# Attention value products with the exponentials as the held operand, in a hybrid Fourier, attention and delta-rule layer

## The chip, the cores and the metric

The kernel runs on one core of a Trainium2 chip. The metric is the device time of one execution in microseconds; several runs are made, and their median is the kernel's time. Engines are called by their roles: TensorE (PE, with its weight loads as PEld), VectorE (DVE), ScalarE (ACT), GpSimd (POOL) and SyncE (SP), which here issues nearly all DMAs.

## The reference, cut to what matters

One layer of a generator on 1024 latent positions and 256 context positions, width 1024, all in float32. A combined input projection feeds a Fourier group, a group of 8 query heads on 2 key/value heads, and a Gated DeltaNet group; the three are concatenated into one output projection, and a squared-ReLU MLP follows. The change touches the attention group alone:

```python
def _attend(q, k, v):
    B, L, _, D = q.shape
    nb = L // QBLK
    qb = q.reshape(B, nb, QBLK, ATT_HKV, ATT_GROUP, D).transpose(1, 0, 2, 3, 4, 5)
    scale = D ** -0.5

    def blk(qi):
        s = jnp.einsum('bqhgd,bkhd->bhgqk', qi, k, preferred_element_type=jnp.float32) * scale
        p = jax.nn.softmax(s, axis=-1).astype(v.dtype)
        return jnp.einsum('bhgqk,bkhd->bqhgd', p, v)
...
    k_all = jnp.concatenate([P['ak'], Pc['ak']], axis=1)
    v_all = jnp.concatenate([P['av'], Pc['av']], axis=1)
    o_att = _attend(P['aq'], k_all, v_all)
```

There are 1024 queries and 1280 keys per head, with 64 channels.

## The kernel before

Most products run in a reduced-precision float32 type with operands split in a high and a low part, so that a product of full precision is a sum of two or three products. `rbase` and the `z1a`, `z1c`, `z2b` zones hold such operands in SBUF, `fbase` and the other zones plain float32; the PSUM banks are `A3` (three, `ba` in the profile) and `bk` (five).

The kernel goes through stages in order of program: modulation and input projection, the delta-rule systems, the attention steps, the output projection, and the MLP's two products (by a seven-product scheme). Attention is a loop of `NPR * 5` = 160 steps. There are 32 query groups `j` of 256 queries (4 groups for each of 8 heads, `h = j // 4`), and each has 5 steps `k2` of two key blocks of 128 keys. A step `n` runs, in this order:

- `side()`, from step `FIRST` = 2 to `LATE` = 145: one piece of other work, first the delta rule's scan (`scan`, many products of 32 or 64 rows on `bk[3]` and `bk[4]`), then the Fourier group (`spectra`);
- `values(n)`: the value products of this step, added up over the 5 steps in the bank `pvs[j % 2]` (`A3[2]` or `bk[2]`);
- `scores(n + LA)`, three steps ahead: four score products, the exponential on ScalarE, and its split into a high part (ScalarE) and a low part (VectorE or GpSimd) in `hl`, with keys on partitions;
- a piece of `maxima` (row maxima for the group two further on), now and then the transposes of `q_T` and `k_T`, and one entry of the list `later`;
- at `k == 4`, `finish(j)`.

In `values`, `VH` and `VL` (the values' high and low parts, 64 channels and a column of ones or zeros) are held, and the exponentials move: high and low side by side in one product of 512 columns on `VH`, the high part alone in one of 256 columns on `VL`. The output has channels on partitions, 0 to 63, and the sum of exponentials on partition 64. `finish` adds the two halves and sends the row of sums to memory; `divide` (after each pair of heads, and after each query group of the last pair) fetches the sums back spread over partitions, takes reciprocals, stores them, fetches them back broadcast, and puts the multiplies and splits into `later`. The result goes to `catAr`, channels on partitions, for the output projection.

A scheduler orders each engine's instructions with its own estimate of times; while `pinned` is set, which holds for all attention steps, TensorE's products and transposes stay in the order of the program (`pe`). `mm` issues one product, `tp` one transpose (a product with the identity).

Of the kernel before, what the change touches and what calls it, by code (L numbers as in the profile page):

```python
# [10 lines left out]
F32 = mybir.dt.float32  # L11
# [3 lines left out]
ALU = mybir.AluOpType  # L15
AX = mybir.AxisListType

P = 128
D = 1024
S = 1024  # L20
# [3 lines left out]
NT = S // P  # L24
NCT = CTX // P
NTA = NT + NCT
HD = 64
CK = 32
VC_ = 68
NCL = S // CK  # L30
NCC = CTX // CK
NCA = NCL + NCC
# [11 lines left out]
PIN = lambda i: i  # L44
# [3 lines left out]
DEFER = 4  # L48
# [143 lines left out]
def body(tc, t, out):  # L192
# [3 lines left out]
    with ctx:  # L196
# [11 lines left out]
        dram = ctx.enter_context(tc.tile_pool(name="scratch", bufs=1, space=bass.MemoryType.DRAM))  # L208
# [4 lines left out]
        def buf(*shape, top=False, a=None, at=None):  # L213
            return Buf(a or Fa, (P,) + shape, top, at)

        def rbuf(*shape, a=None):
            return Buf(a or Ra, (P,) + shape)

        def act(o, i, f=AF.Copy, **k):
            return SC.activation(o, i, f, **k)  # L220

        def f32(ap):
            return ap.bitcast(F32)
# [8 lines left out]
        def mm(o, l, r, start, stop):  # L232
            pe(T.matmul(o, l, r, start=start, stop=stop))  # L233
# [6 lines left out]
        def tp(o, i):  # L240
            pe(T.transpose(o, i, C["ident"]))
# [173 lines left out]
        for k, _ in enumerate(mod_steps(0, slabs, bk[2])):  # L415
            b = trb.next()
# [247 lines left out]
        b = gb.next()  # L664
# [236 lines left out]


        catA = [rbuf(4, S) for _ in range(2)]
        ab = dict(identr=rbuf(P), vlh=rbuf(NTA, 2, VC_), mr=[rbuf(2, VC_) for _ in range(2)], kv=buf(NTA, 2, HD), q=[buf(NT, HD) for _ in range(2)], p=[buf(512) for _ in range(2)], st=[buf(8) for _ in range(6)])
        qr, pr, str_, mrr = (Ring(ab[k]) for k in ("q", "p", "st", "mr"))
        ptr_ = Ring([bk[0], bk[1]])
        ld = [[dram.tile([2, S], F32, name=f"l{w}{q}") for q in range(4)] for w in "ab"]
        catAr = [b() for b in catA]
        VH, VL = (ab["vlh"]()[:, :, w, 0 : HD + 1] for w in range(2))
        identr = ab["identr"]()  # L910
        V.tensor_copy(identr, C["ident"])
        for m_ in ab["mr"]:
# [9 lines left out]
        V.tensor_copy(VH[:, :, HD], C["ones"][:, 0:NTA])  # L922
        V.tensor_scalar(VL[:, :, HD], C["ones"][:, 0:NTA], 0.0, None, op0=ALU.mult)
        s1r = Ring(A3[0:2])
        pvs = [A3[2], bk[2]]
        KVr = ab["kv"]()
# [73 lines left out]

        def values(n):
            k2, hl, pv = n % 5, pt.pop(n), pvs[n // 5 % 2]
            for kk in range(2):
                kb = k2 * 2 + kk
                if kb == 9:
                    mm(pv[0 : HD + 1, 0:256], VL[:, kb], hl[:, kk, 0], False, False)
                mm(pv[0 : HD + 1], VH[:, kb], hl[:, kk].rearrange("p a b -> p (a b)"), kb == 0, kb == 9)
                if kb < 9:
                    mm(pv[0 : HD + 1, 0:256], VL[:, kb], hl[:, kk, 0], False, False)

        def finish(j):
            h, gq = j // 4, j % 4
            if j % 8 == 0:
                o2[h // 2] = o2r.next()()
            O2 = o2[h // 2]
            r = slice(64 * (h % 2), 64 * (h % 2) + 64)
            cs_ = slice(gq * 256, gq * 256 + 256)
            o1, lr = o1r.next()(), lrr.next()()
            pv = pvs[j % 2]
            act(o1[0:65], pv[0:65, 256:512])  # L1020
            V.tensor_tensor(O2[r, cs_], pv[0:64, 0:256], o1[0:64], op=ALU.add)
            V.tensor_tensor(lr[64:65], pv[64:65, 0:256], o1[64:65], op=ALU.add)
            la, lb_ = (x[h // 2] for x in ld)
            Y.dma_start(la[h % 2 : h % 2 + 1, cs_], lr[64:65])

            def divide(n, c0, eng, pin=pe):
                li, rl = lir.next()()[0 : n // 8], rlr.next()()[:, c0 : c0 + n]
                zs = slice(c0, c0 + n)
                Y.dma_start(li, la[:, zs].rearrange("h (p q) -> h p q", q=16))
                V.reciprocal(li, li)  # L1030
                Y.dma_start(lb_[:, zs].rearrange("h (p q) -> h p q", q=16), li)
                for z in range(2):
                    Y.dma_start(rl[64 * z : 64 * z + 64], lb_[z : z + 1, zs].to_broadcast([64, n]))
                for c in range(c0, c0 + n, 256):
                    cs_, ch, cl = slice(c, c + 256), *(x[:, h // 2, c : c + 256] for x in catAr)

                    def mul(cs_=cs_, ch=ch, c=c):
                        pin(eng.tensor_tensor(O2[:, cs_], rl[:, c - c0 : c - c0 + 256], O2[:, cs_], op=ALU.mult))
                        (pe if n < S else PIN)(act(ch, O2[:, cs_]))

                    def sub(cs_=cs_, ch=ch, cl=cl):
                        pin(eng.tensor_tensor(cl, O2[:, cs_], f32(ch), op=ALU.subtract))

                    later.extend((mul, sub))

            if j // 4 == NPR // 4 - 1:
                later.extend([None] * DEFER)
                divide(256, gq * 256, V)
            elif j % 8 == 7:
                later.extend([None] * 5)  # L1050
                divide(S, 0, G)

        NPR, LA = 32, 3

# [40 lines left out]
        for b in fst.items + wb + [thb]:  # L1095
# [2 lines left out]
        zp1, Z1 = zone("left", Z1W, F32, "z1b")  # L1098
        ab.update(
            kT=[rbuf(S + CTX) for _ in range(2)], qT=[rbuf(S) for _ in range(2)], qm=[rbuf(256) for _ in range(3)], hl=[rbuf(2, 2, 256) for _ in range(3)],  # L1100
            o2=[buf(S) for _ in range(2)], rl=[buf(S)],
        )
        ab["p"].append(buf(512, top=True))
        ab.update(o1=[buf(256) for _ in range(2)], lr=[buf(256)], li=[buf(16) for _ in range(3)])
        qTr, qmr, hlr, o1r, o2r, lrr, rlr, lir = (Ring(ab[k]) for k in ("qT", "qm", "hl", "o1", "o2", "lr", "rl", "li"))
        kset.append([x() for x in ab["kT"]])
        one_row(1)
        q_load(1)
# [695 lines left out]
```

## Time and profile before

| what | value |
| --- | --- |
| runs | 1458.84, 1454.71, 1459.01 us; median 1458.84 |
| profiled execution | 1456.26 us, span 1454.5 us |
| TensorE busy | 1384.1 us (95%), 11462 products |
| weight loads busy | 1117.6 us (77%) |
| VectorE, ScalarE, GpSimd busy | 1005.7, 703.6, 668.5 us |
| mean granted TensorE clock | 0.985 |

Times in views count from the start of the span. The name `ba<-rbase` gives the tile written and those read; `128*65 128x512` is 128 rows by 65 held columns, and 512 moving columns on 128 partitions. A product's recorded duration includes a latency that overlaps its neighbours, so a group's length is not the sum of its rows.

### The profile page before, as it was taken

The page shows a single profiled execution, that of the slowest core. Times are in us where ns is not written, and L with a number is a line of the kernel's source. Part 1 is how long each engine was busy: PE and PEld are TensorE (multiplying, and loading weights), DVE is VectorE, ACT ScalarE, POOL GpSimd, SP SyncE. Part 2 cuts the span into 40 slices and gives each one's busy share as a digit, 9 for nine tenths or more (in the row PEclk, how much of TensorE's full clock was granted, in tenths as well). Part 3 has the DMA queues.
Part 4 walks back from the last instruction along what each step waited for, and adds up shares of the span by engine and source line. Part 5 has one row for each costly group of instructions (what it writes and reads, how often), then busy time and mean ns, then how long its engine had stood idle before and what let it go on. Part 6 is the DMA issues. An engine that isn't in the chain of part 4 may idle for free.

```text
span 1454.5 us, 28942 instructions
## 1 busy us (share of the span) xinstructions
PE 1384.1 (95%) x11462; PEld 1117.6 (77%) x11462; DVE 1005.7 (69%) x1695; ACT 703.6 (48%) x1239; POOL 668.5 (46%) x739
## 2 busy tenths in 40 slices
PE   4899988989999999989899899999999999999997
PEld 1677977766777777778799777888888888888886
DVE  0774679986878877786633887655556576776984
ACT  1742422323777777776412654554545443443331
POOL 2653679973446466374433733444443100010782
PEclk8999999999999999999999999999999999999999
DMA  8973141242000010042322315544446898766641
GB/s 316 334 257 125 45 118 44 53 93 76 9 10 24 9 38 4 17 142 80 95 84 91 106 55 183 168 147 134 141 151 217 307 392 269 245 230 215 197 157 58
DMA packets 137304, 197.67 MB, mean 136 GB/s; under 512 B 45021, under 2 KB 80463, under 8 KB 136911
## 3 DMA queue, kind: packets, MB, share of 16 engines
q1 hardware_dynamic: 136464, 195.12, 41.0%
q8 instruction: 90, 1.47, 0.4%
q10 hardware_dynamic: 703, 0.69, 0.2%
q14 instruction: 47, 0.39, 0.1%
HBM read 149.84 MB, written 45.94 MB: 135 GB/s over the span
## 4 chain that ended last, share of the span: by engine, by line
PE 47%; DVE 2%; POOL 2%; DMA 1%; issue 1%; ACT 1%; SPq 0%; DVEq 0%; POOLq 0%; ACTq 0%
PE bk L237 8%; PE bk L238 8%; PE bk L236 8%; PE ba L236 7%; PE ba L237 7%; PE ba L238 7%; PE bk L233 1%; DVE z1b L1335 0%; PE ba L233 0%; DMA fbase<-w_out 0%; POOL rbase L1470 0%; DMA fbase<-la 0%; DMA la<-fbase 0%; DVE rbase L998 0%; POOL z2c L1734 0%
## 5 line engine op out<-in xcount | busy, mean ns | idle before, releaser
L220 ACT ACTIVATE rbase<-fbase 128x512 fp32r<-128x512 f32 (+3 forms) x255 | 171.4, 685 | 87.5 <-PE bk L237 54.8
L220 ACT ACTIVATE fbase<-bk 128x512 f32<-128x512 f32 (+3 forms) x224 | 124.9, 561 | 150.8 <-PE bk L233 81.0
L233 PE MATMUL bk<-rbase 128*128 128x256 f32 (+2 forms) x984 | 173.3, 311 | 4.4 <-ACT fbase L220 2.6
L233 PEld LDWEIGHTS bk<-rbase 128*128 128x128 f32 (+1 forms) x984 | 132.3, 175 | 34.1 <-ACT fbase L220 3.4
L220 ACT ACTIVATE z1c<-fbase 128x512 fp32r<-128x512 f32 (+1 forms) x120 | 76.8, 653 | 138.5 <-DMA fbase<-w_ff 51.8
L233 PE MATMUL ba<-rbase 128*65 128x512 f32 (+4 forms) x576 | 138.4, 343 | 5.6 <-DVE rbase L998 4.8
L1503 POOL TENSOR_TENSOR fbase<-fbase 128x512 f32<-128x512 f32 x64 | 87.4, 1366 | 114.4 <-DVE z1c L1470 81.2
L220 ACT ACTIVATE fbase<-fbase 128x512 f32<-128x512 f32 (+4 forms) x148 | 95.9, 659 | 90.6 <-POOL fbase L1626 27.2
L1708 POOL TENSOR_TENSOR z2c<-z2c,fbase 128x512 f32<-128x512 f32 x16 | 31.1, 1969 | 203.8 <-ACT z2c L220 127.9
L974 DVE TENSOR_REDUCE fbase<-ba 128x1 f32<-128x512 f32 (+1 forms) x192 | 106.4, 593 | 19.6 <-PE ba L233 18.3
L220 ACT ACTIVATE rbase<-z1d 128x1024 fp32r<-128x1024 f32 x61 | 63.0, 1055 | 101.9 <-PE bk L237 81.8
L1470 DVE TENSOR_TENSOR z1c<-fbase,z1c 128x512 fp32r<-128x512 f32 x112 | 91.5, 820 | 23.6 <-ACT z1c L220 19.7
L1470 DVE TENSOR_TENSOR rbase<-z1d,rbase 128x1024 fp32r<-128x1024 f32 x61 | 84.9, 1407 | 31.1 <-ACT rbase L220 30.9
L998 POOL TENSOR_TENSOR rbase<-fbase,rbase 128x512 fp32r<-128x512 f32 x56 | 72.1, 1287 | 67.2 <-ACT rbase L220 63.0
L236 PE MATMUL bk<-rbase 128*128 128x512 f32 x256 | 99.7, 389 | 0.0
L237 PE MATMUL bk<-rbase 128*128 128x512 f32 x256 | 99.7, 389 | 0.0
L238 PE MATMUL bk<-rbase 128*128 128x512 f32 x256 | 99.6, 389 | 0.0
L998 DVE TENSOR_TENSOR rbase<-fbase,rbase 128x512 fp32r<-128x512 f32 x104 | 80.5, 774 | 25.7 <-ACT rbase L220 25.3
L1470 DVE TENSOR_TENSOR rbase<-fbase,rbase 128x1024 fp32r<-128x1024 f32 (+1 forms) x65 | 81.0, 1265 | 21.8 <-ACT rbase L220 21.6
L233 PEld LDWEIGHTS ba<-rbase 128*65 128x65 f32 (+1 forms) x576 | 76.2, 155 | 23.3 <-DVE rbase L998 5.9
L238 PE MATMUL ba<-rbase 128*128 128x512 f32 x192 | 74.8, 389 | 0.0
L237 PE MATMUL ba<-rbase 128*128 128x512 f32 x192 | 74.7, 389 | 0.0
(349 smaller groups left out, 3815.8 us busy)
## 6 DMA issues: line engine op xcount, KB each, us to landing
fbase<-w_ff SPq DMA_DIRECT2D x70, 512.0 KB
u<-fbase SPq DMA_DIRECT2D x112, 256.0 KB
z2a<-w_mod SPq DMA_DIRECT2D x36, 512.0 KB
z1d<-w_ff SPq DMA_DIRECT2D x34, 512.0 KB
z1d<-u SPq DMA_DIRECT2D x33, 512.0 KB
fbase<-u SPq DMA_DIRECT2D x23, 512.0 KB
fbase<-w_in SPq DMA_DIRECT2D x16, 512.0 KB
fbase<-x SPq DMA_DIRECT2D x14, 512.0 KB
```

The costliest lines, as they stand in the source:

```text
L220: return SC.activation(o, i, f, **k)
L233: pe(T.matmul(o, l, r, start=start, stop=stop))
L236: pe(T.matmul(o, lh, rh, start=start, stop=False))
L237: pe(T.matmul(o, lh, rl, start=False, stop=False))
L238: pe(T.matmul(o, ll, rh, start=False, stop=stop))
L974: V.tensor_reduce(st4[:, z : z + 1], b, AX.X, ALU.max)
L998: (G if k2 in GP and not any(a <= n < b for a, b in NGP) else V).tensor_tensor(hl[:, :, 1], p, f32(hl[:, :, 0]), op=ALU.subtract)
L1470: eng.tensor_tensor(lo, i, f32(hi), op=ALU.subtract)
L1503: G.tensor_tensor(w[nm], w[a], w[b], op=op)
L1708: G.tensor_tensor(c, c, G2[cs_.start // 512], op=ALU.mult)
```

## The change

`values` now holds the exponentials, 128 queries at a time, and moves the values. `V2` has for each key block 132 columns: `VL`, `VH`, a one, a zero. The high exponentials meet 130 columns (`VL`, `VH`, the one, the zero), the low ones 66 (`VH`, the one, the zero); per key block that is two products of each, for the two halves of the 256 queries. The output has queries on partitions: per query 64 channels of the `VL` product, 64 of the `VH` products, and the sum of exponentials. `finish` adds the two, takes the reciprocal of the sum and multiplies there; every second head, `turn`, one entry of `later` further on, transposes the pair of heads back into the same bank and splits it into `catAr`. `divide`, its DMAs and its scratch tensors are gone.

```diff
         def values(n):
             k2, hl, pv = n % 5, pt.pop(n), pvs[n // 5 % 2]
+            pvq = pv.rearrange("p (q c) -> p q c", q=2)
             for kk in range(2):
                 kb = k2 * 2 + kk
-                if kb == 9:
-                    mm(pv[0 : HD + 1, 0:256], VL[:, kb], hl[:, kk, 0], False, False)
-                mm(pv[0 : HD + 1], VH[:, kb], hl[:, kk].rearrange("p a b -> p (a b)"), kb == 0, kb == 9)
-                if kb < 9:
-                    mm(pv[0 : HD + 1, 0:256], VL[:, kb], hl[:, kk, 0], False, False)
+                for w in (0, 1) if kb < 9 else (1, 0):
+                    for q in range(2):
+                        l = hl[:, kk, w, q * P : (q + 1) * P]
+                        mm(pvq[:, q, w * HD : 2 * HD + 2], l, V2[:, kb, w * HD : 2 * HD + 2], kb == w == q == 0, kb == 9 and w == 0 and q == 1)
 
         def finish(j):
...
-            act(o1[0:65], pv[0:65, 256:512])
-            V.tensor_tensor(O2[r, cs_], pv[0:64, 0:256], o1[0:64], op=ALU.add)
-            V.tensor_tensor(lr[64:65], pv[64:65, 0:256], o1[64:65], op=ALU.add)
-            la, lb_ = (x[h // 2] for x in ld)
-            Y.dma_start(la[h % 2 : h % 2 + 1, cs_], lr[64:65])
-
-            def divide(n, c0, eng, pin=pe):
...
+            act(o1, pvq[:, :, 0:HD])
+            V.reciprocal(ri, pvq[:, :, 2 * HD])
+            V.tensor_tensor(o1, pvq[:, :, HD : 2 * HD], o1, op=ALU.add)
+            O2 = o2[h // 2][:, gq * 2 : gq * 2 + 2]
+            V.tensor_tensor(O2[:, :, h % 2], o1, ri.unsqueeze(2).to_broadcast([P, 2, HD]), op=ALU.mult)
+            if h % 2:
+                cs_ = slice(gq * 256, gq * 256 + 256)
+                ch, cl = (x[:, h // 2, cs_] for x in catAr)
+
+                def turn():
+                    b = pv[:, 0:256]
+                    for q in range(2):
+                        tp(b[:, q * P : (q + 1) * P], O2[:, q].rearrange("p a d -> p (a d)"))
+                    act(ch, b)
+                    V.tensor_tensor(cl, b, f32(ch), op=ALU.subtract)
+
+                later.extend((None, turn))
```

TensorE's instructions in one attention step and the start of the next, with the bank `ba_75` collecting the value products, `bk_77` and `bk_76` taking scores, `ba_73` and `ba_74` the maxima, and `bk_79`, `bk_80` the scan. Before:

```order
L233 MATMUL bk_77<-rbase 128x256 x4
L233 MATMUL ba_73<-rbase 128x256
L233 MATMUL ba_74<-rbase 128x512
L233 MATMUL bk_79<-z1b,z2a 32x64 x8
L233 MATMUL ba_75<-rbase 65x512
L233 MATMUL ba_75<-rbase 65x256
L233 MATMUL ba_75<-rbase 65x512
L233 MATMUL ba_75<-rbase 65x256
L233 MATMUL bk_76<-rbase 128x256 x4
```

The same place in the changed program (lines are one further on; shapes are those of the output, and x2 means two in a row):

```order
L234 MATMUL bk_77<-rbase 128x256 x4
L234 MATMUL ba_73<-rbase 128x256
L234 MATMUL ba_74<-rbase 128x512
L242 MATMUL bk_78<-fbase 128x128 x2
L234 MATMUL bk_79<-z1b,z2a 32x64 x8
L234 MATMUL ba_75<-rbase 128x130 x2
L234 MATMUL ba_75<-rbase 128x66 x2
L234 MATMUL ba_75<-rbase 128x130 x2
L234 MATMUL ba_75<-rbase 128x66 x2
L234 MATMUL bk_76<-rbase 128x256 x4
```

Four value products have become eight, and the two transposes of a `turn` (L242, on the bank `bk_78` of an earlier group) stand between the maxima and the scan; all else keeps its place.

VectorE's instructions at a `finish` of the bank `bk_78`, up to two steps later, before:

```order
L1021 TENSOR_TENSOR fbase<-bk_78,fbase 64x256
L1022 TENSOR_TENSOR fbase<-bk_78,fbase 1x256
L998 TENSOR_TENSOR rbase<-fbase,rbase 128x2x256
L974 TENSOR_REDUCE fbase<-ba_73 128x1
L974 TENSOR_REDUCE fbase<-ba_74 128x1
L1215 TENSOR_TENSOR z1b<-bk_79,z1b 128x2x64
```

And now, with the split of the turned result (L1034) at the end:

```order
L1021 RECIPROCAL fbase<-bk_78 128x2
L1022 TENSOR_TENSOR fbase<-bk_78,fbase 128x128
L1024 TENSOR_TENSOR fbase<-fbase 128x2x64
L999 TENSOR_TENSOR rbase<-fbase,rbase 128x2x256
L975 TENSOR_REDUCE fbase<-ba_73 128x1
L975 TENSOR_REDUCE fbase<-ba_74 128x1
L1200 TENSOR_TENSOR z1b<-bk_79,z1b 128x2x64
L1200 TENSOR_TENSOR z1b<-bk_80,z1b 128x2x64
L975 TENSOR_REDUCE fbase<-ba_73 128x1
L975 TENSOR_REDUCE fbase<-ba_74 128x1
L977 TENSOR_REDUCE rbase<-fbase 128x1
L1181 SCALAR_TENSOR_TENSOR z1b<-bk_79,fbase,z2a 128x64 x2
L1034 TENSOR_TENSOR rbase<-bk_78,rbase 128x256
```

The two sums have become a reciprocal, a sum and a multiply, and the split stands ten instructions behind the multiply (L1024).

More of the change, by code (lines that the diff above doesn't have):

```diff
@@ L1024, in finish @@
-            Y.dma_start(la[h % 2 : h % 2 + 1, cs_], lr[64:65])
-            def divide(n, c0, eng, pin=pe):
[L1027 to L1051, printed above, removed]
+            pvq = pv.rearrange("p (q c) -> p q c", q=2)
+            o1, ri = o1r.next()(), rir.next()()
+            act(o1, pvq[:, :, 0:HD])
+            V.reciprocal(ri, pvq[:, :, 2 * HD])
+            V.tensor_tensor(o1, pvq[:, :, HD : 2 * HD], o1, op=ALU.add)
+            O2 = o2[h // 2][:, gq * 2 : gq * 2 + 2]
@@ L1100, in body @@
             kT=[rbuf(S + CTX) for _ in range(2)], qT=[rbuf(S) for _ in range(2)], qm=[rbuf(256) for _ in range(3)], hl=[rbuf(2, 2, 256) for _ in range(3)],
[L1101 removed]
+            o2=[buf(NT, 2, HD) for _ in range(2)],
         )
         ab["p"].append(buf(512, top=True))
[L1104 to L1105 removed]
+        ab.update(o1=[buf(2, HD) for _ in range(2)], ri=[buf(2) for _ in range(2)])
+        qTr, qmr, hlr, o1r, o2r, rir = (Ring(ab[k]) for k in ("qT", "qm", "hl", "o1", "o2", "ri"))
         kset.append([x() for x in ab["kT"]])
```

15 lines of the change are left out of this document (6 added, 9 removed).

## The prediction

> **What bounds the kernel now.** I read the summary of the page first, then busy time by stretches around the attention stage, then TensorE's groups kept apart by shape, then single moments in order of time.
>
> ```profile
> PE 1384.1 (95%) x11462; PEld 1117.6 (77%) x11462; DVE 1005.7 (69%) x1695; ACT 703.6 (48%) x1239; POOL 668.5 (46%) x739
> PE 47%; DVE 2%; POOL 2%; DMA 1%; issue 1%; ACT 1%; SPq 0%; DVEq 0%; POOLq 0%; ACTq 0%
> ```
>
> TensorE is busy for 95% of the span and holds nearly all of the chain that ended last. The attention steps run from about 351 us to 719 us (the last L1021, quoted further down). By stretches (columns: length, then busy time and instruction count of each engine, clock, DMA):
>
> ```profile
> 351.00:630.00 279.00, 275.84 (x4251) 210.25 (x4250) 219.97 (x539) 206.92 (x427) 144.81 (x187) 1.00 0.09 27
> 630.00:660.00 30.00, 26.43 (x154) 21.80 (x153) 23.20 (x39) 18.65 (x36) 26.58 (x22) 0.94 0.30 88
> ...
> 690.00:710.00 20.00, 14.57 (x84) 11.09 (x83) 16.86 (x32) 15.16 (x28) 13.58 (x9) 0.91 0.12 35
> ...
> sum 379.00, PE 365.60 PEld 287.26 DVE 290.11 ACT 266.11 POOL 202.45; mean PE 73.12 PEld 57.45 DVE 58.02 ACT 53.22 POOL 40.49
> ```
>
> Up to 630 us TensorE idles 3.2 us of 279, while VectorE is at 79% and ScalarE at 74%: TensorE is the limit there. From 351 to 730 us it idles 379.0 - 365.6 = 13.4 us, of which 5.4 us lie between 690 and 710 us. Since ends of products are modelled, "busy" does not show spacing, so I take spacing from the start of one group to the start of the next:
>
> ```profile
> 523.04 0.91 PE L233 MATMUL ba<-rbase 128*65 128x512 f32 x4
> 523.80 0.28 PE L233 MATMUL bk<-rbase 128*128 128x256 f32 x1
> 699.98 0.86 PE L233 MATMUL ba<-rbase 128*65 128x512 f32 x4
> 700.67 0.28 PE L233 MATMUL bk<-rbase 128*128 128x256 f32 x1
> 620.85 0.65 PE L233 MATMUL bk<-rbase 128*128 128x256 f32 x4
> 621.33 0.29 PE L233 MATMUL ba<-rbase 128*65 128x128 f32 x2
> 625.62 0.60 PE L241 MATMUL bk<-fbase 128*64 128x128 f32 x4
> ```
>
> The first row of each pair is the four value products of a step (two of 512 columns, two of 256, all with 65 held columns); the second is the first score product behind them. So the value products of a step take 0.76 us when small products of the side work stand ahead (523.04 to 523.80), and 0.69 us when nothing of the kind does (699.98 to 700.67).
>
> ```profile
> L233 PE MATMUL bk<-rbase 128*128 128x256 f32 x200 | 52.5, 283 | 0.2 <-DVE rbase L942 0.2
> L233 PE MATMUL ba<-rbase 128*65 128x128 f32 x40 | 5.7, 224 | 0.0
> L241 PE MATMUL bk<-fbase 128*64 128x128 f32 x50 | 7.6, 272 | 0.0
> L233 PEld LDWEIGHTS bk<-rbase 128*128 128x128 f32 x200 | 37.9, 190 | 8.1 <-DVE rbase L942 0.6
> L233 PEld LDWEIGHTS bk<-rbase 128*65 128x65 f32 x200 | 22.3, 136 | 8.9
> L233 PEld LDWEIGHTS bk<-z1b 32*64 32x64 f32 x528 | 10.6, 132 | 6.3 <-ACT rbase L220 2.2 <-issue 2.1 <-ACT fbase L220 0.4
> L233 PEld LDWEIGHTS bk<-z1b,fbase 32*32 32x32 f32 x992 | 16.0, 104 | 10.7 <-issue 3.5 <-DVE z1b L1161 1.7 <-DVE z1b L1215 1.4
> L241 PEld LDWEIGHTS bk<-fbase 128*64 128x64 f32 x50 | 5.5, 111 | 0.7
> ```
>
> These are the means by shape between 400 and 620 us. Four score products in 0.65 us with a last one of 283 ns are (650 - 283) / 3 = 122 ns apart; the two products of 128 moving columns are 290 - 224 = 66 ns apart; four transposes are (600 - 272) / 3 = 109 ns apart. The decisive rows are the weight loads: 104 ns for 32 held columns, 136 for 65, 190 for 128. That is (190 - 104) / 96 = 0.90 or (190 - 136) / 63 = 0.86 ns a column, so streaming 128 columns takes 110 to 115 ns; the remaining 75 ns or so is latency that overlaps, since products with 136 ns loads stand 66 ns apart.
>
> **The change, part by part.** *Value products.* Per key block two products become four, each with its own load of 128 held columns, with 130, 130, 66 and 66 columns moving. Moving columns per block fall from 768 to 392, which alone would be a gain. But a load overlaps only the product before it, and a product of 66 or 130 columns is over in at most about 66 ns (the row of 128 columns), less than a load's 110. So each of the eight products of a step costs a load. Bounds for that spacing: 110 ns from below, by the slope; 122 ns from above, by the score products, which have the same loads and also 256 columns to stream. I take 113, nearer to the slope, because the moving side no longer binds.
>
> A step with side work ahead then takes one exposed load and eight spacings, 0.110 + 8 x 0.113 = 1.014 us instead of 0.755: +0.259. A step without takes 8 x 0.113 = 0.904 instead of 0.69: +0.214. Side work precedes steps FIRST = 2 to LATE = 145, so 143 steps x 0.259 + 17 x 0.214 = 37.0 + 3.6 = +40.7 us. With 110 it is +36.8, with 122 it is +52.2.
>
> The Trainium skill (TensorE: Matmul & The Clock Gate, section Back-to-back issue gap) gives about 81 ns for a sustained pair of load and product of 128 columns. No row here shows such a pair with 128 held columns; by 81 ns the value products would cost about as much as before. It is one of the rivals below.
>
> *Transposes.* 32 are added (two in each of 16 calls of `turn`), 32 x 0.109 = +3.5 us. The order puts each pair where TensorE changes from wide to small products anyway, so I add no further switch. They wait for the division on VectorE. Behind them in TensorE's queue stand the scan's products and the next step's values; everything would wait with them. The order gives the division about ten VectorE instructions of lead, and `turn` runs two steps after `finish`, some 4 us at (719 - 351) / 160 = 2.3 us a step, so I cost this wait at nothing; without that cover it costs up to 1 us in each of 16 places (a rival).
>
> *Vector, scalar and pool work.*
>
> ```profile
> L1021 DVE TENSOR_TENSOR fbase<-ba,fbase x16: 415/417/420, 361.0 to 704.8; 64x256 f32<-64x256 f32 x16
> L1021 DVE TENSOR_TENSOR fbase<-bk,fbase x16: 406/418/419, 371.7 to 719.1; 64x256 f32<-64x256 f32 x16
> L1022 DVE TENSOR_TENSOR fbase<-ba,fbase x16: 422/422/423, 361.4 to 705.2; 1x256 f32<-1x256 f32 x16
> L1030 DVE RECIPROCAL fbase<-fbase x7: 240/242/253, 436.3 to 725.1; 32x16 f32<-32x16 f32 x4, 128x16 f32<-128x16 f32 x3
> L1042 DVE TENSOR_TENSOR rbase<-fbase,rbase x4: 400/418/930, 702.6 to 731.3; 128x256 fp32r<-128x256 f32 x4
> L1215 DVE TENSOR_TENSOR z1b<-bk,z1b x80: 273/281/293, 359.8 to 614.2; 128x128 f32<-128x128 f32 x80
> L1038 POOL TENSOR_TENSOR fbase<-fbase x12: 727/737/1185, 447.7 to 650.0; 128x256 f32<-128x256 f32 x12
> ```
>
> VectorE loses 32 x (0.42 + 0.42) = 26.9 us and gains 32 x (at most 0.24 for a reciprocal of two columns, 0.28 for the sum, 0.28 for the product) + 16 x 0.42 for the low halves = 32.3 us. The last query groups lose their VectorE multiplies and seven reciprocals. Net a few us on an engine at 79%, covered by TensorE's longer steps: 0. ScalarE keeps one copy per group and 16 rounded copies: 0. GpSimd loses 12 multiplies of 0.74 us and about as many subtracts, nothing that TensorE waits for. The copies of the setup are of the same size: 0.
>
> *DMA.* The 32 small stores of sums and the seven round trips through memory go. SP's queue gets shorter, and loads of `x`, the tables and `w_out` move forward. In the window no product waits for a DMA, so that is worth 0. The last round trip (704 to 731 us) lies under output-projection products that the scheduler put ahead. What TensorE does wait for:
>
> ```profile
> PE ba L233 <- DVE rbase L998: 4.8, 4, 1.9
> PE bk L238 <- DVE z2b L1304: 1.9, 1, 1.9
> PE bk L233 <- DVE rbase L998: 1.6, 2, 1.0
> ```
>
> The largest waits are for the low halves of the exponentials (L998), late because VectorE is crowded by other work near 690 us. Longer steps give VectorE time to catch up, so part of the 13.4 us of idle time is filled instead of added to. I take 6 us: about 25 steps after 630 us that each grow by 0.2 could fill most of the 10 us there, but the two clusters are bursts. Bounds 2 and 10.
>
> *Sum*: 40.7 + 3.5 - 6 = +38.2 us against the profiled execution of 1456.26 us (span 1454.5), 1494.5. That execution lies 2.6 us under the median of the runs, 1458.84; in terms of the median I forecast 1496 us, slower by 2.5%. About 0.3% is what a measurement can tell from no change here.
>
> **The rivals.**
> - *Loads of the exponentials run faster than the slope.* Transposes show a faster load: 111 ns for 64 held columns, and
>
> ```profile
> L241 PEld LDWEIGHTS bk<-fbase,z1b x16: 137/141/144, 687.9 to 695.2; 128*128 128x128 f32 x16
> ```
>
> that is (141 - 111) / 64 = 0.47 ns a column, 60 ns for 128. If the new loads ran like this, the spacing would be about 66 ns, a step 0.06 + 8 x 0.066 = 0.59 us, and the sum 143 x -0.165 + 17 x -0.16 + 3.5 = -23 us: 1436. It decides below about 80 ns, where the terms cancel. Against it: all loads of the non-transposed products lie on the slow slope, those of 128 columns too. 6%.
> - *Loads at some 81 ns*, between the two: a step of 0.08 + 8 x 0.081 = 0.73 us, -4 + 3.5 us, so no change, 1459. The same rows speak against it. 4%.
> - *The load's latency is no longer hidden behind so short a product.* Then the spacing is the whole 190 ns, a step 8 x 0.190 = 1.52 us or a little over, 143 x 0.77 + 17 x 0.83 + 3.5 = +128 us: 1587. Against it: products with 136 ns loads 66 ns apart. 4%.
> - *The turn waits for the division, or VectorE becomes the limit.* 16 waits of 1 us on top of the forecast: 1512. VectorE at 79% speaks for some such waits, the lead in the order against it. 9%.
>
> **How the numbers follow.** The forecast has the remaining 77%. Its own ends: 110 ns with 10 us filled gives 36.8 + 3.5 - 10 = +30, 1489; 122 ns with 2 us filled gives 52.2 + 3.5 - 2 = +54, 1513. I set the range from 1478 to 1516: upward it takes in the waits of the turn, downward some more filled idle time; the two fast rivals and the slow one, 14% together, stay outside. Faster 7%, within 0.3% 4%, slower 89%.
>
> **What would show it.** In the changed profile value products with 128 held columns should start 110 to 122 ns apart, a step's eight taking about 1.0 us; their loads should have the 190 ns of the score loads; TensorE's load row should rise from 75% to over 80% of the time between 351 and 630 us, and the attention stage should end some 35 us later, with later stages as long as before. Value products 66 to 81 ns apart would make the forecast wrong, as would idle TensorE ahead of the new transposes, or an attention stage in which VectorE and not TensorE is without gaps.

## The result, and the profile after

The changed kernel takes 1512.57 us (median of four runs: three from 1507.11 to 1517.12 and one of 3484.64), the kernel before 1457.96 beside it: a ratio of 1.0369, 95% interval 1.0347 to 1.0391. The forecast was 1496 us in a range from 1478 to 1516, so direction and range held, and 16 us were missed (12 by 1508.01, the median of the three). Medians here and below count every run, and ratios leave out the disturbed ones, which are one of four here, one of six in late_turn, one of seven in kept66 and three of six in kept130.

The comparison below is of the profiled executions, 1507.11 us (span 1505.3, mean granted clock 0.974) against 1456.26 (span 1454.5, 0.985): 50.8 us of span. First the page after: busy times, TensorE's share by fortieths of the span, and the granted clock in the same slices.

```profile
PE 1444.4 (96%) x12134; PEld 1208.7 (80%) x12134; DVE 1009.1 (67%) x1728; ACT 702.8 (47%) x1239; POOL 645.4 (43%) x715
...
PE   5899988999999999999999989999999999999997
...
PEclk9999998999999899988989999999999999999999
```

The clock's row of the page before:

```profile
PEclk8999999999999999999999999999999999999999
```

TensorE has become busier and its clock has more slices below nine tenths; these are the two parts of the result. The first part is seen in one step (rows in order of time: start, length, engine, group). TensorE's products, then its weight loads:

```profile
375.38 1.08 PE L234 MATMUL ba<-rbase 128*128 128x130 f32 x8
376.30 0.72 PE L234 MATMUL bk<-rbase 128*128 128x256 f32 x4
376.86 0.52 PE L234 MATMUL ba<-rbase 128*128 128x256 f32 x2
```

```profile
375.38 0.97 PEld L234 LDWEIGHTS ba<-rbase 128*128 128x128 f32 x8
376.27 0.54 PEld L234 LDWEIGHTS bk<-rbase 128*128 128x128 f32 x4
```

From the first value product to the first score product it is 0.92 us where the step at 523.04 us of before showed 0.76. Eight loads in 0.97 us with a last one of some 192 ns (the row below) are (0.97 - 0.19) / 7 = 0.111 us apart. The loads by shape, 504 to 660 us:

```profile
L234 PEld LDWEIGHTS bk<-rbase 128*128 128x128 f32 x364 | 50.4, 192 | 2.5
L234 PEld LDWEIGHTS ba<-rbase 128*128 128x128 f32 x330 | 42.6, 191 | 3.2 <-DVE fbase L975 0.4 <-issue 0.2
```

A load of 128 exponentials is recorded with the same 191 ns as a load of the scores' operand. The second part, the clock, stands in the attention stage cut at its changes (length; busy time and count of PE, PEld, DVE, ACT, POOL; clock; DMA):

```profile
351.00:490.00 139.00, 137.75 (x2005) 119.08 (x2004) 103.74 (x257) 91.28 (x187) 56.52 (x73) 1.00 0.04 8
490.00:506.00 16.00, 15.02 (x149) 12.94 (x148) 7.07 (x20) 6.02 (x12) 3.98 (x6) 0.57 0.00 1
506.00:667.00 161.00, 159.31 (x2596) 136.95 (x2595) 109.47 (x287) 104.25 (x220) 65.19 (x89) 1.00 0.09 26
667.00:687.00 20.00, 17.73 (x78) 16.33 (x79) 13.45 (x25) 10.76 (x20) 17.00 (x13) 0.57 0.32 112
687.00:744.00 57.00, 56.05 (x431) 53.87 (x430) 41.73 (x79) 38.75 (x68) 19.72 (x16) 1.00 0.23 74
744.00:772.00 28.00, 26.58 (x158) 25.73 (x158) 15.59 (x23) 12.26 (x22) 14.05 (x9) 0.70 0.19 58
...
sum 429.00, PE 420.45 PEld 372.90 DVE 293.41 ACT 264.62 POOL 178.18; mean PE 60.06 PEld 53.27 DVE 41.92 ACT 37.80 POOL 25.45
```

The clock is either full or half. Three of these stretches are at half for most of their length, and in each the half clock begins at or behind a wait of TensorE, shown in brackets here:

```profile
491.18 0.83 PE L234 MATMUL bk<-z1b,z2a 64*32 64x64 f32 x16 [0.98 <-DVE z1b L1200]
669.26 1.39 PE L234 MATMUL ba<-rbase 128*128 128x256 f32 x2 [2.37 <-DVE fbase L975]
745.78 0.44 PE L242 MATMUL bk<-fbase 128*128 128x128 f32 x2 [1.42 <-DVE fbase L1024]
```

The first waits for the scan's state, the second for a row maximum, the third is a `turn` that waits for its division. Before had such waits as well, two of which lead to half clock (two single moments, then two stretches):

```profile
643.26 0.39 PE L238 MATMUL bk<-z2b 128*128 128x256 f32 x1 [1.86 <-DVE z2b L1304]
...
702.75 0.91 PE L233 MATMUL ba<-rbase 128*65 128x512 f32 x4 [1.44 <-DVE rbase L998]
```

```profile
643.00:650.00 7.00, 6.74 (x38) 6.12 (x39) 3.20 (x7) 3.48 (x5) 6.75 (x6) 0.76 0.34 112
...
704.00:712.00 8.00, 7.36 (x43) 6.02 (x42) 5.36 (x8) 6.01 (x12) 7.36 (x5) 0.79 0.28 86
```

There 7 x 0.24 and 8 x 0.21 us of clock are missing; at half clock the time is twice that, 3.4 us each. After, the same sum gives 16 x 0.43 = 6.9, 20 x 0.43 = 8.6 and 28 x 0.30 = 8.4 us missing, that is 14, 17 and 17 us at half clock. The clock's own records give 13.65, 17.07 and 13.65 us, four to five times the 3.41 us of before; the third stretch holds 3.41 us more, at 768 us, with no wait ahead of it.

### The profile page after: what moved, and what is told of

Its sections match the earlier page's. It is cut to its first block, busy times and chain, and to the rows that moved or that the text cites. A ratio compares the mean times of both kernels' runs of the same rounds, so it can differ in the third digit from the quotient of the medians.

```text
span 1505.3 us, 30196 instructions
## 1 busy us (share of the span) xinstructions
PE 1444.4 (96%) x12134; PEld 1208.7 (80%) x12134; DVE 1009.1 (67%) x1728; ACT 702.8 (47%) x1239; POOL 645.4 (43%) x715
## 4 chain that ended last, share of the span: by engine, by line
PE 73%; DVE 5%; POOL 5%; ACT 2%; issue 2%; DMA 0%; SPq 0%; DVEq 0%; POOLq 0%; ACTq 0%
PE bk L234 15%; PE bk L237 8%; PE bk L239 8%; PE bk L238 8%; PE ba L237 8%; PE ba L238 8%; PE ba L239 8%; PE ba L234 7%; POOL z2a L762 2%; POOL fbase L761 1%; PE bk L242 1%; DVE fbase L761 1%; ACT rbase L221 1%; DVE rbase L999 1%; ACT fbase L221 1%
## 5 line engine op out<-in xcount | busy, mean ns | idle before, releaser
L234 PE MATMUL bk<-rbase 128*128 128x256 f32 (+4 forms) x1304 | 205.9, 302 | 1.8 <-ACT fbase L221 1.8
L221 ACT ACTIVATE rbase<-fbase 128x512 fp32r<-128x512 f32 (+3 forms) x239 | 165.5, 704 | 78.2 <-PE bk L238 55.5
L234 PEld LDWEIGHTS bk<-rbase 128*128 128x128 f32 (+1 forms) x1304 | 172.6, 201 | 9.1 <-ACT fbase L221 2.5
L234 PE MATMUL ba<-rbase 128*128 128x130 f32 (+4 forms) x896 | 156.3, 302 | 2.9 <-DVE fbase L975 2.4
L234 PEld LDWEIGHTS ba<-rbase 128*128 128x128 f32 (+1 forms) x896 | 122.6, 196 | 11.0 <-DVE fbase L975 3.3
```

## The experiments

The table has, for each kernel, the median over the steps at full clock and without a wait of the time from the first value product to the fourth score product (read from single records of the trace, for steps with small products of the side work ahead); for the attention stage of the profiled execution, from the first score product to the last, its length, TensorE's idle time in it, the clock time missing in it (half of what ran at half clock) and the rest, which is TensorE's work at full clock; and the measured time and ratio to before. The clock is counted in attention alone, because the stages ahead of it lose 11.9 to 22.2 us of clock in every kernel, without a relation to the change (15.4 in before, 11.9 in after, 20.5 in again).

| kernel | value products of a key block | step, us | attention, us: length = idle + clock missing + rest | time, us | ratio, 95% interval |
| --- | --- | --- | --- | --- | --- |
| before | held 65; 512 + 256 columns move | 1.111 | 368.0 = 13.1 + 3.4 + 351.5 | 1457.96 | |
| after | held 128; 130, 130, 66, 66 | 1.360 | 425.4 = 8.6 + 22.2 + 394.6 | 1512.57 | 1.0369 (1.0347 to 1.0391) |
| again (after, unchanged) | the same | 1.360 | 423.9 = 8.6 + 20.5 + 394.8 | 1504.87 | 1.0326 (1.0303 to 1.0349) |
| pad130 | held 128; 4 x 130 | 1.359 | 405.9 = 5.0 + 6.8 + 394.1 | 1488.00 | 1.0210 (1.0196 to 1.0224) |
| pad192 | held 128; 4 x 192 | 1.358 | 401.5 = 5.1 + 1.7 + 394.7 | 1491.20 | 1.0238 (1.0225 to 1.0251) |
| pad256 | held 128; 4 x 256 | 1.409 | 407.2 = 4.8 + 0.0 + 402.4 | 1496.58 | 1.0277 (1.0264 to 1.0290) |
| late_turn | as after | 1.358 | 423.8 = 8.9 + 22.2 + 392.7 | 1506.40 | 1.0337 (1.0295 to 1.0378) |
| split8 | held 65; 128, 128, 256, 256 | 1.125 | 370.1 = 12.7 + 3.3 + 354.1 | 1454.54 | 0.9990 (0.9980 to 1.0000) |
| held64 | held 64; 130, 130, 66, 66 | 0.950 | 361.7 = 22.2 + 3.4 + 336.1 | 1454.97 | 0.9977 (0.9955 to 0.9999) |
| held128 | held 128, then 65 (values); 256, 256 | 0.939 | 369.3 = 28.5 + 10.9 + 329.9 | 1457.58 | 1.0007 (0.9996 to 1.0017) |
| held128b | the same, VectorE lighter | 0.940 | 372.2 = 32.2 + 12.9 + 327.1 | 1460.51 | 1.0028 (1.0018 to 1.0038) |
| held128c | the same, lighter still | 0.937 | 371.0 = 32.0 + 13.2 + 325.8 | 1458.28 | 1.0012 (1.0001 to 1.0022) |
| kept66 | as after, all engines' order kept | 1.358 | 618.7 = 13.9 + 238.9 + 365.9 | 1659.65 | 1.1386 (1.1345 to 1.1428) |
| kept130 | as pad130, all engines' order kept | 1.359 | 530.9 = 24.2 + 117.8 + 388.9 | 1633.78 | 1.1024 (1.0974 to 1.1075) |

**again.** No edit: the changed kernel on the chip of the next experiments.

> The changed kernel itself, beside the next three on the same chip. 1505 to 1517 us. Theory: of the 51 us it lost, about 40 come from loads of 128 held columns at 112 ns each and about 18 from TensorE's clock, granted at half for some 48 us of the attention stage (7 us before the change), less some idle time that was filled. So clock at half for 35 us or more between 350 and 780 us again.

1504.87 us, runs from 1496.44 (granted clock 0.976) to 1508.44 (0.967). The medians of the two sets of runs of this kernel differ by 8 us (by 3 without the run of 3484.64), and in both the longer runs by and large have the lower clock, down to 0.960 at 1517.12. The step is the same, and attention again has 41 us at half clock, where 35 or more were expected.

**pad192 and pad256: more columns move behind each load.** In both kernels all four value products of a key block move 192 or 256 columns; the added ones (low values for the low exponentials, and parts of the next key block) land in columns of the bank that `finish` does not read, or add the product of the two low parts:

```
-  mm(pvq[:, q, w * HD : 2 * HD + 2], l, V2[:, kb, w * HD : 2 * HD + 2], ...)
+  c0 = kb * VW
+  mm(pvq[:, q, 0:192], l, V2f[:, c0 : c0 + 192], ...)
```

> Each of the eight value products of a step moves 192 columns instead of 130 or 66 (the rest are values of the next key block or zeros, added into columns of the bank that nobody reads; the low exponentials also meet the low values). Held columns and number of products are unchanged. Loads-and-clock theory: 192 columns stream in about 80 ns, under the 112 ns of a load, so the loads' spacing stays 112 ns; TensorE streams for 71% of the time instead of 37%, the clock stays at half for less than 20 us of the attention stage, and the kernel gets 8 to 18 us faster than the changed one, 1490 to 1500 us. Rival, moved columns set the time: 8 x 94 columns more in each of 160 steps at 0.42 ns, +50 us or more, 1555. Rival, the clock follows idle gaps alone: no change, 1505 to 1512, clock at half as long as in the changed kernel.

> The same with 256 moved columns for each value product, as many as the score products have. Loads-and-clock theory: spacing 112 to 122 ns as for the score products, so 0 to 13 us more at full clock, and clock at half for under 15 us of the attention stage, -15 us or more: 1490 to 1507 us. Rival, moved columns set the time: 8 x 158 columns more per step at 0.42 ns, +85 us. Rival, the clock follows idle gaps alone: 1505 to 1520 with clock at half as long as in the changed kernel.

With 192 columns the step is 1.358 us, unchanged, though 768 columns move per key block instead of 392; with 256 it is 1.409, 6 ns more a product. So up to 192 columns the load sets the spacing and the moved columns cost nothing: the prediction's reason for the loss holds. As both texts expected, the kernels that move more are faster than the changed kernel, with intervals well apart: their attention misses 1.7 and 0.0 us of clock, again's 20.5.

**pad130: the smallest padding.** All four products take 130 columns, so the low exponentials meet the low values too:

```
-  mm(pvq[:, q, w * HD : 2 * HD + 2], l, V2[:, kb, w * HD : 2 * HD + 2], ...)
+  mm(pvq[:, q, 0 : 2 * HD + 2], l, V2[:, kb, 0 : 2 * HD + 2], ...)
```

> The changed kernel with 130 moved columns for all eight value products (the low exponentials also meet the low values). Loads-and-clock theory: spacing stays 112 ns, TensorE streams for 48% of it instead of 37%, and the time at half clock lies between that of the changed kernel and that with 192 columns: 1495 to 1508. Rival, moved columns set the time: 4 x 64 columns more per step at 0.42 ns, +17 us, 1525.

1488.00 us, 17 us faster than the runs of again with 128 more columns moved per key block, and faster than expected. Its attention in two stretches, to be compared with the clocks of 0.57 and 0.70 above:

```profile
351.00:630.00 279.00, 278.17 (x4340) 240.66 (x4342) 205.07 (x518) 182.71 (x380) 118.43 (x156) 1.00 0.05 13
630.00:720.00 90.00, 87.39 (x872) 80.86 (x871) 68.42 (x134) 62.76 (x118) 44.69 (x38) 1.00 0.28 91
```

The step did not get shorter; the clock stayed full up to 720 us (one stretch at half clock, 13.65 us long, follows at 730). Of the 18.0 us by which its attention is shorter than again's, 20.5 - 6.8 = 13.7 are clock and 3.6 idle time. But the scheduler had also ordered VectorE's instructions differently, and the waits at 490 and 667 us were gone.

They are gone in pad192 and pad256 too, but the wait of the last pair's `turn` stands in all of these kernels, and there they can be compared (again, pad130, pad192, pad256):

```profile
745.53 0.44 PE L242 MATMUL bk<-fbase 128*128 128x128 f32 x2 [1.47 <-DVE fbase L1024]
730.57 0.69 PE L242 MATMUL bk<-fbase 128*128 128x128 f32 x2 [1.43 <-DVE fbase L1024]
734.70 0.44 PE L242 MATMUL bk<-fbase 128*128 128x128 f32 x2 [1.47 <-DVE fbase L1029]
740.15 0.44 PE L242 MATMUL bk<-fbase 128*128 128x128 f32 x2 [1.43 <-DVE fbase L1029]
```

Behind this one wait the half clock lasts 10.24 us in again (13.65 in after), 13.65 in pad130, 3.41 in pad192, and it does not come in pad256. So at this wait the step from 66 to 130 columns for the low exponentials shows no gain, and what pad130 gained in clock goes with the two waits that are gone. From 130 to 192 and 256 columns, with nearly the same order of the other engines, the half clock shrinks and goes. This is one execution of each kernel. kept66 and kept130, at the end, ask about columns and order once more.

**late_turn: the turn two entries later.**

```
-  later.extend((None, turn))
+  later.extend((None, None, None, turn))
```

> Only the place of the transposes changes: turn runs four steps after finish instead of two. Theory: the wait of 1.4 us of one turn for its division at 744 us goes, and with it the 14 us at half clock that follow, so 3 to 8 us faster than the changed kernel, 1499 to 1505. Rival: TensorE waits there for VectorE anyway (for the low halves of the exponentials) and the clock falls all the same: within 2 us of the changed kernel.

1506.40 us, no gain that can be told from again (1504.87). The wait for the division is gone, and in its place the value products wait for the turn's split:

```profile
PE ba L234 <- DVE fbase L975: 2.4, 1, 2.4
PE ba L234 <- DVE rbase L1034: 1.7, 1, 1.7
```

At 745 us the clock falls to half all the same, for 13.65 us. The turn works in its group's own bank, which the group after the next needs again, so that a later turn delays that group: the wait moved.

**split8: eight products, but loads of 65 columns.** The kernel before, with the product on `VL` cut in two of 128 columns and that on `VH` in two of 256: eight value products in a step of two key blocks, and the same columns moved:

```
-  mm(pv[0 : HD + 1], VH[:, kb], hl[:, kk]..., kb == 0, kb == 9)
-  mm(pv[0 : HD + 1, 0:256], VL[:, kb], hl[:, kk, 0], False, False)
+  for q in range(2):
+      mm(pv[0 : HD + 1, q * P : (q + 1) * P], VL[:, kb], hl[:, kk, 0, q * P : (q + 1) * P], kb == q == 0, False)
+  for w in range(2):
+      mm(pv[0 : HD + 1, w * 256 : w * 256 + 256], VH[:, kb], hl[:, kk, w], False, kb == 9 and w == 1)
```

> The kernel before, with each value product cut in two by its moving columns: eight products a step with eight loads of 65 held columns, 256 or 128 columns moving. Loads theory: a load of 65 columns streams in 56 ns and stays under its product (118 and 66 ns), so a step grows by 2 x (2 x 118 + 2 x 66 - 347) = 0.04 us, the kernel by 0 to 10 us: 1457 to 1468. Rival, the number of products and loads sets the time: as slow as the changed kernel, about 1510.

1454.54 us, like before and a little under the range expected. One step in order of time:

```profile
374.22 0.92 PE L233 MATMUL ba<-rbase 128*65 128x128 f32 x8
374.98 0.64 PE L233 MATMUL bk<-rbase 128*128 128x256 f32 x4
```

Eight products in the same 0.76 us that four took. The number of products costs next to nothing by itself (1.125 us a step against 1.111).

**held64: half the exponentials held.** Leaves out half of the queries' outputs: each value product holds 64 queries instead of 128.

```
-  l = hl[:, kk, w, q * P : (q + 1) * P]
-  mm(pvq[:, q, ...], l, ...)
+  l = hl[:, kk, w, q * P : q * P + HD]
+  mm(pvq[0:HD, q, ...], l, ...)
```

> The changed kernel with only 64 of each 128 queries held (half of the attention outputs are left out; the other half of each result is whatever stands in the bank): eight products a step, the same moved columns, half the held columns. Loads theory: a load streams in 56 ns, the products are 60 to 66 ns apart, a step drops from 1.00 to about 0.55 us for its value products, the kernel by 50 to 75 us: 1432 to 1458, unless VectorE (then near 88%) holds it back by some us. Rival, a fixed cost per product: no change, 1505 to 1512.

The step falls by 0.41 us to 0.950, which for 160 steps would be 66 us; the time falls by 50 against again. So the loads of 128 columns are what the change costs, and with short loads the value products would have been cheaper than before. Over attention TensorE's work at full clock falls by 394.8 - 336.1 = 58.7 us and the missing clock by 17.1; against that TensorE idles 13.6 us more, in waits for VectorE of which the changed kernel had fewer (waited for; total, times, longest):

```profile
PE ba L234 <- DVE fbase L975: 4.4, 9, 1.7
PE bk L234 <- DVE z1b L1181: 2.8, 6, 0.9
```

**held128, held128b, held128c: full loads of values under long products.** The kernel before with the values held, but high and low values in one load of 128 columns that meets the high exponentials, and the high values alone for the low ones, two products of 256 moving columns (leaves out the low part of one of 64 channels in each head, whose place the sum of exponentials takes). held128b moves a copy of `finish` to ScalarE and two small pieces to GpSimd, held128c in addition gives GpSimd three of five low halves of the exponentials instead of two.

```
+  mm(pv[0 : (P, HD + 1)[w], w * 256 : w * 256 + 256], (VA, VB)[w][:, kb], hl[:, kk, w], kb == w == 0, kb == 9 and w == 0)
```

```
-  V.tensor_copy(vl[0:64], pv[64:128, 0:256])
+  act(vl[0:64], pv[64:128, 0:256])
-  V.tensor_tensor(O2[r, cs_], vl[0:64], o1[0:64], op=ALU.add)
+  G.tensor_tensor(O2[r, cs_], vl[0:64], o1[0:64], op=ALU.add)
```

> The kernel before with the values still held, but as 128 columns (64 high parts, a one, 63 low parts) that meet the high exponentials in one product of 256 moved columns, and the first 65 of them meeting the low ones in another: two products per key block, 512 moved columns instead of 768. It leaves out the low part of one of the 64 value channels of each head. Loads theory: held columns are free up to the product's own length, so the four products take 4 x 0.118 = 0.47 us, plus 0.06 for a longer first load, instead of 0.755: -0.2 us in 160 steps, less some extra VectorE work in 32 places: 1415 to 1440. Rival: ScalarE and VectorE (74% and 79% busy before) take over as the limit and give most of it back: 1440 to 1458.

> held128 (values held, 128 columns of high and low values in one load, two products of 256 moved columns per key block; leaves out the low part of one of the 64 channels of each head), with the copy of the output's second half moved from VectorE to ScalarE, and the clearing of one row and the last sum to GpSimd. Theory: held128 saved TensorE 0.17 us a step and lost it to VectorE; with some 35 us less on VectorE the waits for its maxima (L975) shrink, 1425 to 1448 us, faster than before. Rival (the rest is lost elsewhere, in ScalarE or the clock): 1450 to 1460.

> held128b, with the low halves of three of five exponential pieces subtracted on GpSimd instead of two of five, VectorE lighter by about another 20 us. Theory: as held128b or up to 10 us faster, 1418 to 1445 us. Rival: GpSimd is now late with the low halves that TensorE needs, 1450 or more.

All three come out at before's time within 0.3%, where the theory had 10 us and more of gain: a miss, at about the times that the rivals named. The gain on TensorE is there, 160 x (1.111 - 0.939) = 27.5 us by the steps without a wait and 351.5 - 329.9 = 21.6 over all of attention, and is given back twice. The first part of attention in held128, then in held128c:

```profile
351.00:630.00 279.00, 262.48 (x4227) 213.95 (x4225) 241.91 (x611) 201.31 (x420) 143.19 (x184) 0.98 0.08 22
```

```profile
351.00:630.00 279.00, 263.56 (x4259) 217.72 (x4259) 215.43 (x519) 215.52 (x455) 205.21 (x264) 0.98 0.10 28
```

In held128 TensorE idles 28.5 us in attention where before idled 13.1, 15.4 more, and the missing clock grows from 3.4 to 10.9 us, 7.5 more. Together they take 22.9 us, a little more than the 21.6 saved. VectorE at 241.91 of 279 us looks like the new limit, and the waits agree (held128, then held128b):

```profile
PE ba L233 <- DVE fbase L975: 10.1, 20, 1.8
PE ba L233 <- DVE rbase L999: 3.7, 4, 1.4
```

```profile
PE ba L233 <- DVE fbase L975: 9.1, 21, 2.4
PE bk L237 <- POOL z2b L1300: 7.6, 4, 4.7
PE ba L233 <- DVE rbase L999: 3.3, 3, 2.0
```

But with VectorE relieved (215.43 us in held128c, less than before's 219.97) TensorE idles no less than in held128, 32.0 us. So VectorE's total is not the reason, and neither is GpSimd, the rival for held128c, late with the low halves: that shows as one wait of 1.2 us. What paces these steps stays open; the order in which VectorE gets to the maxima was not tried.

**kept66 and kept130: columns or order?** The changed kernel and pad130, each with the instructions of VectorE, ScalarE and GpSimd kept in the order of the program during the attention steps, as TensorE's already are. The two differ in nothing but the moved columns (66 or 130 for the low exponentials).

```
+                return lambda *a, **k: tc.keep_in_program_order(f(*a, **k))
...
+        V, G, SC = Kept(nc.vector), Kept(nc.gpsimd), Kept(nc.scalar)
```

> The changed kernel with 66 moved columns for the low exponentials, but with the instructions of VectorE, ScalarE and GpSimd kept in the order of the program during the attention steps, as TensorE's are. It is the partner of kept130, which differs from it only in moved columns, so that no other engine's order differs between the two. Theory (short products leave the array with little to stream, and half clock lasts long after a wait): first value product to fourth score product 1.36 us at full clock, at least 30 us at half clock within attention, and kept66 at least 6 us slower than kept130. Rival (the wider products were faster only because the other engines' orders came out differently): the two agree within 4 us.

> kept66 with 130 moved columns in all eight value products (the low exponentials meet the low values too, which the reference's precision does not need). All engines' orders are those of kept66. Theory: steps of 1.36 us at full clock all the same, but less time at half clock, so at least 6 us faster than kept66 though it streams more. Rival: within 4 us of kept66.

kept66 took 1651 to 1704 us in 7 runs at granted clocks of 0.885 down to 0.847, kept130 1596 to 1664 us in 6 runs at 0.931 down to 0.874. The medians are 26 us apart in the direction of the theory, but the runs overlap, so that these runs alone do not settle it. The profiled executions, kept66's slowest and kept130's third fastest, show how far two runs can part. Both wait 1.10 us at the same place of the program, a product of the maxima that waits for VectorE, kept66 first:

```profile
357.48 0.38 PE L247 MATMUL ba<-rbase 128*128 128x256 f32 x1 [1.10 <-DVE fbase L223]
```

```profile
358.31 0.38 PE L247 MATMUL ba<-rbase 128*128 128x256 f32 x1 [1.10 <-DVE fbase L223]
```

and then, in the 90 us that follow (kept66, then kept130):

```profile
360.00:450.00 90.00, 89.96 (x681) 77.24 (x681) 35.50 (x96) 34.37 (x68) 20.74 (x28) 0.50 0.02 4
```

```profile
360.00:450.00 90.00, 84.17 (x1046) 70.05 (x1047) 56.18 (x150) 53.54 (x108) 32.53 (x43) 1.00 0.03 8
```

kept66 falls to half clock and stays there, 98.99 us without a break, with TensorE recorded as busy throughout. kept130 goes on at full clock, although it waits 5.8 us in these 90. A step at half clock reads like this in kept66:

```profile
395.22 1.91 PE L247 MATMUL ba<-rbase 128*128 128x130 f32 x8
396.95 1.20 PE L247 MATMUL bk<-rbase 128*128 128x256 f32 x4
```

1.73 us to the first score product instead of 0.92. Where the clock is full, both kernels have the steps of after and pad130 (1.358 and 1.359). So at equal order, in this pair, fewer moved columns meant the longer half clock behind this wait; later kept130 has half clock too, up to 68 us without a break. The order matters more: against after and pad130 the kept order costs over 100 us, nearly all of it clock missing in attention (238.9 against 22.2, 117.8 against 6.8 us), which is more than the columns are worth.

## Why the prediction was right or wrong

The 50.8 us of span, term by term:

| term | predicted | measured | from |
| --- | --- | --- | --- |
| value products | +40.7 | +39.8 | 160 x (1.360 - 1.111) |
| transposes | +3.5 | +3.5 | 32 x 0.109, their spacing in the trace |
| granted clock | no term | +18.8 | 22.2 - 3.4 us of clock missing in attention |
| idle time filled | -6 | -4.5 | 8.6 - 13.1 us in attention |
| the rest | 0 | -6.8 | what is left |

**The load sets the spacing: right.** 113 ns was taken from the slope of recorded loads, 111 to 112 was measured. All three other spacings are excluded, 66, 81 and 190 ns. One detail differs: the load that is not hidden lies mostly not ahead of the first value product but behind the last (from the first score product to the second it is 204 ns in the step at 375.38 us, where the step at 523.04 us of before had 118), and the step's 1.014 us counted it once either way. split8 and held64 show the same from the other side: eight products with short loads cost next to nothing, and halving the held columns takes 0.41 us off a step. The Trainium skill (TensorE: Matmul & The Clock Gate, section LDWEIGHTS) gives columns / 1.2 ns, 107 for 128, and the traces agree within 5 ns; its 81 ns for a pair (section Back-to-back issue gap), the rival of 4%, doesn't hold for these operands.

**Vector, scalar, pool work and DMA at nothing: right in the sum, with one wrong size.** VectorE stays at 1009.1 us against 1005.7. But the multiply of the division was priced at 0.28 us, and it is

```profile
L1024 DVE TENSOR_TENSOR fbase<-fbase x32: 291/652/2084, 360.9 to 773.3; 128x128 f32<-128x128 f32 x32
```

(shortest, median, longest in ns). The trace shows what goes with the long ones: the 23 of the 32 that take over 300 ns all begin while an instruction of GpSimd runs, and end 146 to 151 ns after the end of that one. Of the nine of 291 to 293 ns, five meet no instruction of GpSimd at their start, three meet one that ends before them, and one overlaps GpSimd throughout.

**No term for the clock: the step that was missing.** The prediction cost TensorE's time as a sum of spacings at the clock of before. The rows for the opposite were on its page: the stretches with idle time had clocks of 0.94 and 0.91, those without had 1.00. What it left out is that three waits of 1 to 2.4 us, which are 4.8 us by themselves, bring half clock for 14 to 17 us each, where before came back after 3.4. In the profiled execution, forecast at 1494.5 and measured at 1507.11, the sum is 12.6 us short: 18.8 of clock and 1.5 of idle time that was not filled, less 0.9 of the value products and 6.8 of the rest. That the measured time still fell into the range is in part luck: its upper end was set for waits of the turn, and the clock took that room. The changed kernel's runs range over 21 us (1496.44 to 1517.12, both sets), by and large in the order of their granted clocks (0.976 to 0.960), while 23 runs of the kernel before stay within about 7.

**The turn's wait at nothing: wrong once in 16.** One `turn`, of the last pair of heads, waits 1.42 us for its division (L1024), and half clock follows: between the sum and the multiply VectorE runs four other instructions (L1320, 1.72 us from 743.23 us on), and the multiply then takes 0.75 us itself. The rival with 16 such waits named 1512 us, the measured median, but for a cause that is not there: 15 of the 16 don't wait.

**Idle time filled, and the rest.** TensorE's idle time in attention fell from 13.1 to 8.6 us, so 4.5 of the 6 us predicted are seen. Of the -6.8 us of the table's last row, 1.1 are an earlier start of attention and 5.5 a shorter stretch behind its last score product (740.4 us, before 745.9), from which 48 products of the output projection have moved forward into attention. At 0.118 us each, their spacing in before, these are 5.7 us; so inside attention the other terms come out some 6 us lower than their sum, and where is not assigned. A part is that missing clock overstates its cost: kept66, with nearly the same products in attention as the changed kernel, misses 216.7 us more clock there, but its rest is 28.7 us smaller.

**What was to be seen.** The load row rose from 75% to 236.93 / 279 = 85% in the same window, as foretold. The last finish moved from 719.1 to 772.9 us, by 54 and not 35: clock again. What follows it is 732.4 us long, before 735.4.

```profile
351.00:630.00 279.00, 275.22 (x4177) 236.93 (x4177) 195.28 (x499) 177.48 (x369) 111.75 (x150) 0.98 0.04 12
```

```profile
L1021 DVE RECIPROCAL fbase<-bk x16: 159/170/172, 372.4 to 772.9; 128x2 f32<-128x2 f32 x16
```

## What to carry to other kernels

Count held columns, not moved ones, when products are short: with 128 held columns these products stood 112 ns apart whether they moved 66 or 192 columns, so the operand that is moved in long rows should be the large one. When a change thins out what TensorE streams, look at the granted clock of each stretch before taking old spacings over, and at each wait of a microsecond as something that may be followed by several times its length at half clock. And ask of a gain on the busiest engine who is next: the 22 us of TensorE's work saved in held128 came back as idle time and missing clock.

## What the runs showed of the hardware that was not expected

- Half clock can outlast the wait that precedes it, and lasted longer where the array streamed less. A load-bound step streams 2 x 392 value columns in eight loads' time; after such waits half clock lasted 14 to 17 us in the changed kernel, 3.4 us in the kernel before, and up to 99 us in kept66 with TensorE recorded as busy all the time. At one and the same wait it lasted 13.65, 3.41 and 0 us with 130, 192 and 256 moved columns. Streaming is not all of it: kept130 moves as much as pad130 and had up to 68 us. The Trainium skill (TensorE: Matmul & The Clock Gate, section What's actually happening) has full clock come back after one busy window of about 3.4 us and fall after an idle one of that length. The traces agree on the grain, since the shortest half-clock stretches are 3.41 us and the longer ones (13.65, 17.07, 98.99) multiples of that, but not on the rule: waits of 0.98 to 2.37 us were enough for the fall, and a busy queue wasn't enough for the return. What counts as busy was not settled here.
- More work can be less time: pad130 moves a third more value columns than the changed kernel and takes 17 us less. By its trace that goes with two waits that another order of VectorE's instructions removed; pad192 and pad256, which move about twice as much and more, have less half clock at the wait that is left as well.
- The same order of TensorE's work in attention, with the other engines in another order, ran 1504.87 and 1659.65 us. At full clock its steps were the same within 2 ns.
